# FFN in 512-token blocks, output projection and half of the convolution between its steps, one product for the head norms

## The chip, the cores and the metric

The kernel runs on one core of a Trainium2 chip. Its time is in device microseconds (us) of one execution. TensorE (PE) multiplies matrices and transposes, VectorE (DVE), ScalarE (ACT) and GpSimd (POOL) do elementwise work, and the queue of SyncE (SP) issues the DMA transfers.

## The reference

One layer of a streaming encoder, on 2048 prompt tokens and 32 tokens of a second stream that has 1024 cached tokens; model width 1024, all in float32.

```python
def layer(x, past_k, past_v, conv_state, ffn_state, ...):
    xn = rmsnorm(x, g_mix)
    q, k, v, u, gate = split(xn @ w_in)            # five times 512 columns
    q = head_rmsnorm(q, g_q); k = head_rmsnorm(k, g_k)   # 8 heads of 64
    o = sb_attend(q, k_all, v_all, ...)            # stick-breaking attention
    c = u * sigmoid(gate)
    c, new_conv_state = causal_dwconv(c, conv_state, w_dw, b_dw)   # 31 taps, 512 channels
    c = silu(layernorm(c, g_conv_ln, b_conv_ln))
    h = x + concatenate([o, c]) @ w_out            # 1024 x 1024
    up = rmsnorm(h, g_ffn) @ w_up                  # 1024 x 5632
    up_c, new_ffn_state = causal_dwconv(up, ffn_state, w_ffn_dw, b_ffn_dw)   # 3 taps
    a, g = split(up_c)                             # twice 2816
    y = h + (silu(g) * a) @ w_down                 # 2816 x 1024
    return y, k, v, new_conv_state, new_ffn_state
```

## The kernel before

Every matmul operand is split into a high part, rounded to float32r by ScalarE, and a low remainder, which VectorE gets by a subtraction (`split`). A product is three matmuls, high by high, high by low and low by high (`mm3`). All tiles lie in two large buffers, `arena` (float32) and `arena_r` (the split operands); `SLOTS` says where, by the name of a tile, and a name has as many buffers as it has places.

The order of the work isn't that of the code. Each helper (`mm`, `tr`, `act`, `vec`, `pool`, `dma`) adds a step to a list with an engine, an estimated price in ns and a rank, which is its place in the program unless one is set by hand. `Plan.run` then walks through time by these prices: an engine that is free takes the ready step of the lowest rank, and a step that opens one of the 8 banks of PSUM needs a free bank, which its rule for banks gives (the last bank only to the oldest tile). What comes out is one fixed stream for each engine, which takes its instructions in that order on the chip. All DMAs go through the queue of SyncE, also in that order. Since all engines' instructions are recorded in the helpers, a row shows the helper's line: L380 is a matmul, L387 a transpose, L394 ScalarE, L409 VectorE or GpSimd, L434 a DMA; the names of the tiles tell which step it is.

The stages, in the order of the program:
- Input projection, to about 565 us: the tokens' two halves, of each first u and gate (`ug`), then k, q and v (`nat`) in column tiles of 256. For q and k, `nat` squares (ScalarE), sums over a head (VectorE), takes the power -1/2 (GpSimd, `rstd_of`), scales each of 8 pieces of 64 columns by its norm (ScalarE, eight instructions), multiplies by the gain (GpSimd), splits and transposes. The gated u stays in `cb`, and `conv` runs the 31 taps on VectorE over 1024 tokens at a time. Its rank is set late, behind all attention, so that it fills VectorE's free time; by the trace it is done at about 564 us.
- Attention, to about 1096 us: `UNITS` of one head and 256 queries, with sigmoids on ScalarE, running products (scans) on VectorE and two matmuls on TensorE.
- Output projection, to about 1307 us: w_out is split once, into the `wo0` and `wo1` tiles; `out_chunk` then takes two token tiles of 128 at a time: reads the heads' output (oT_d) and the convolution (yT_d), normalises, multiplies, adds x and writes h to `h_d`. The last chunk has three tiles (the third is the second stream's 32 tokens), with the weights as the stationary side and a transpose behind.
- FFN, the rest: `SEGS` are 768, 640 and 640 + 32 tokens. `norm_seg` reads h back, scales it by norm and gain on VectorE, transposes and splits. For each of 22 tiles of 128 hidden columns `up` loads and splits two tiles of w_up (one for a, one for g), in every segment anew, multiplies in two column halves into two banks, runs the 3 taps on VectorE, SiLU, the product and a split, and loads and splits a tile of w_down. After each two of them `down` multiplies and adds to y.

## Time and profile before

| | before |
|---|---|
| runs | 2819.62 us median of 3 (2814.54 to 2824.38) |
| profiled execution | 2816.1 us, span 2814.2 us, mean granted clock 0.992 |
| busy | PE 2690.4 us (96%), DVE 2003.1 (71%), ACT 1103.1 (39%), POOL 494.3 (18%) |
| DMA | 288.29 MB, mean 102 GB/s |
| chain that ended last | PE 73%, DVE 10%, issue 6%, POOL 6%, ACT 3%, DMA 2% |

The span is the time from the first to the last instruction of the profiled execution; its own time is 1.9 us longer. Busy shares are means over stages that differ: which engine limits a stage is read from that stage's stretch. Idle time stands beside the engine whose result ended it.

### The profile page before, as it was taken

The page shows a single profiled execution, that of the slowest core. Times are in us where ns is not written, and L with a number is a line of the kernel's source. Part 1 is how long each engine was busy: PE and PEld are TensorE (multiplying, and loading weights), DVE is VectorE, ACT ScalarE, POOL GpSimd, SP SyncE. Part 2 cuts the span into 40 slices and gives each one's busy share as a digit, 9 for nine tenths or more (in the row PEclk, how much of TensorE's full clock was granted, in tenths as well). Part 3 has the DMA queues.
Part 4 walks back from the last instruction along what each step waited for, and adds up shares of the span by engine and source line. Part 5 has one row for each costly group of instructions (what it writes and reads, how often), then busy time and mean ns, then how long its engine had stood idle before and what let it go on. Part 6 is the DMA issues. An engine that isn't in the chain of part 4 may idle for free.

```text
span 2814.2 us, 43546 instructions
## 1 busy us (share of the span) xinstructions
PE 2690.4 (96%) x17345; PEld 2527.0 (90%) x17345; DVE 2003.1 (71%) x2311; ACT 1103.1 (39%) x2179; POOL 494.3 (18%) x724
## 2 busy tenths in 40 slices
PE   8999999988888888999999999999999999999999
PEld 8999999977777877889999999999999999999998
DVE  6988888899989998345565656666666665656566
ACT  5267235566666675114222222322232233322222
POOL 1155035523223231011000000000000001101100
PEclk9999999999999999999999999999999999999999
DMA  4255224644333335555222222242222233222221
GB/s 161 64 177 175 76 82 152 192 130 116 85 93 85 93 99 159 182 159 170 68 60 68 60 63 72 89 159 71 75 83 75 73 99 103 80 73 64 83 61 70
DMA packets 299907, 288.29 MB, mean 102 GB/s; under 512 B 21591, under 2 KB 260077, under 8 KB 298679
## 3 DMA queue, kind: packets, MB, share of 16 engines
q1 hardware_dynamic: 299703, 285.50, 33.3%
q8 instruction: 136, 2.23, 0.3%
q14 instruction: 68, 0.56, 0.1%
HBM read 217.08 MB, written 64.11 MB: 100 GB/s over the span
## 4 chain that ended last, share of the span: by engine, by line
PE 73%; DVE 10%; issue 6%; POOL 6%; ACT 3%; DMA 2%; SPq 0%; POOLq 0%; DVEq 0%; ACTq 0%
PE bank L380 70%; DVE arena L409 6%; POOL few L409 3%; DVE arena_r L409 3%; PE bank L387 3%; POOL arena L409 3%; ACT arena L394 2%; ACT arena_r L394 1%; DMA arena<-in_cache_sb_v_dram 1%; SPq L434 0%; DMA arena<-arena 0%; DVE few L409 0%; DMA oT_d<-arena 0%; DMA arena<-in_w_ffn_dw_dram 0%; DMA qT_d<-arena_r 0%
## 5 line engine op out<-in xcount | busy, mean ns | idle before, releaser
L380 PE MATMUL bank<-arena_r 128*128 128x256 f32 (+8 forms) x15360 | 2494.5, 322 | 32.4 <-DVE arena_r L409 31.0
L380 PEld LDWEIGHTS bank<-arena_r 128*128 128x128 f32 x15360 | 2320.6, 190 | 157.1 <-DVE arena_r L409 43.3
L409 DVE TENSOR_TENSOR arena_r<-arena,arena_r 128x1024 fp32r<-128x1024 f32 (+5 forms) x398 | 421.7, 1068 | 466.2 <-ACT arena_r L394 462.8
L394 ACT ACTIVATE arena_r<-arena 128x1024 fp32r<-128x1024 f32 (+5 forms) x398 | 368.7, 935 | 911.1 <-PE bank L380 509.8
L394 ACT ACTIVATE arena<-bank 128x384 f32<-128x384 f32 (+15 forms) x770 | 327.6, 473 | 278.2 <-PE bank L380 244.4
L409 DVE TENSOR_TENSOR arena<-bank,arena 128x512 f32<-128x512 f32 (+2 forms) x458 | 281.8, 631 | 189.5 <-PE bank L380 189.2
L409 DVE TENSOR_TENSOR_SCAN arena<-arena 128x1024 f32<-128x1024 f32 (+11 forms) x200 | 330.4, 1680 | 15.1 <-ACT arena L394 7.8
L409 DVE SCALAR_TENSOR_TENSOR arena<-arena,wdw 128x1024 f32<-128x1024 f32 (+1 forms) x240 | 320.6, 1367 | 1.6
L387 PE MATMUL bank<-ident,arena 128*128 128x128 f32 (+4 forms) x1645 | 224.0, 279 | 67.2 <-DVE arena L409 50.6
L387 PEld LDWEIGHTS bank<-ident,arena 128*128 128x128 f32 (+4 forms) x1645 | 185.5, 142 | 100.0 <-DVE arena L409 57.0
L409 POOL COPY halo<-arena 128x2 f32<-128x2 f32 x176 | 80.4, 472 | 1061.8 <-ACT arena L394 1049.8
L394 ACT ACTIVATE arena_r<-bank 128x512 fp32r<-128x512 f32 (+4 forms) x422 | 218.2, 570 | 110.5 <-PE bank L387 98.2
L409 DVE SCALAR_TENSOR_TENSOR arena<-arena,wfd 128x768 f32<-128x768 f32 (+2 forms) x264 | 248.1, 940 | 10.2
L409 DVE TENSOR_TENSOR arena_r<-bank,arena_r 128x512 fp32r<-128x512 f32 (+2 forms) x334 | 194.2, 634 | 18.2 <-ACT arena_r L394 18.0
L409 POOL TENSOR_SCALAR_AFFINE_SELECT arena<-arena 128x128 f32<-128x128 f32 (+1 forms) x130 | 132.8, 1032 | 338.5 <-ACT arena L394 338.1
L394 ACT ACTIVATE arena<-arena 128x1024 bf16<-128x1024 f32 (+4 forms) x100 | 88.2, 882 | 254.3 <-DVE arena L409 237.1
L409 POOL TENSOR_SCALAR few<-few 128x1 f32<-128x1 f32 (+3 forms) x87 | 62.1, 713 | 493.1 <-DVE few L409 405.3
L409 POOL TENSOR_TENSOR few<-few,nhalf 128x1 f32<-128x1 f32 (+3 forms) x87 | 112.0, 1290 | 6.6
L409 DVE TENSOR_TENSOR arena<-arena 128x768 f32<-128x768 f32 (+4 forms) x78 | 68.7, 881 | 46.7 <-ACT arena L394 33.2
L394 ACT ACTIVATE arena<-bank,few 128x64 f32<-128x64 f32 (+1 forms) x272 | 68.6, 325 | 77.9 <-POOL few L409 77.9
L409 DVE TENSOR_SCALAR arena<-arena,wfd,bfd 128x768 f32<-128x768 f32 (+2 forms) x132 | 84.0, 637 | 6.0 <-ACT arena L394 6.0
L409 POOL COPY arena<-halo 128x2 f32<-128x2 f32 x132 | 24.5, 185 | 294.1 <-DVE arena L409 281.7
(43 smaller groups left out, 377.8 us busy)
## 6 DMA issues: line engine op xcount, KB each, us to landing
arena<-in_w_up_dram SPq DMA_DIRECT2D x132, 512.0 KB
arena<-in_w_down_dram SPq DMA_DIRECT2D x66, 512.0 KB
arena<-in_x_prompt_dram SPq DMA_DIRECT2D x32, 512.0 KB
arena_r<-qT_d SPq DMA_DIRECT2D x64, 256.0 KB
arena<-h_d SPq DMA_DIRECT2D x32, 512.0 KB
arena<-in_w_in_dram SPq DMA_DIRECT2D x24, 512.0 KB
arena<-in_w_in_dram SPq DMA_DIRECT2D x32, 256.0 KB
out_dram<-arena SPq DMA_DIRECT2D x32, 256.0 KB
```

What stands on the lines that cost most here:

```text
L380: lambda: nc.tensor.matmul(plan.real(out), lhsT, rhs, start=start, stop=stop),
L387: "pe", in_.shape[0] * (0.4167 if in_.dtype == F32R else 0.8333) + 2.5, lambda: nc.tensor.transpose(plan.real(out), in_, idt), [out], [in_ ...
L394: "act", ns, lambda: nc.scalar.activation(out, plan.real(in_), func, **kw), aps(out, kw.get("accum_out")), reads
L409: self.tag, self.price(name, n / (2 if fast else 1), pointers), lambda: fn(out, *map(plan.real, args), **kw), [out], aps(*args, *kw.values())
```

## The change

- The FFN runs over four blocks of 512 tokens (`BLK`, `NBLK`); the second stream's 32 tokens go with the last. An up tile of the first three blocks is one bank of 512 columns, of the last two of 272. In the first block, weights are loaded raw in halves, split as before, and the split tiles stored to DRAM (`wu_d`, `wd_d`); the other blocks load these, 1 MB each.
- The output projection is cut into blocks and into its two halves of input rows: `project(b, 1, ...)` multiplies the convolution, `project(b, 0, ...)` the heads; the second to run adds to what the first wrote to h. Block 0 is projected between attention and FFN (convolution first). Block b + 1 is projected between the steps of block b's FFN, where a generator (`weave`, `upto`) adds its steps to the list (heads first). w_out is split anew in each of these, in the FFN's buffers (`out_weights`).
- The gated u goes to DRAM (`c_d`) instead of `cb`. `conv(b)` works on 512 tokens; blocks 0 and 1 in the input projection (rank behind all attention, as before), blocks 2 and 3 between the steps of the FFN's blocks 1 and 2.
- `norm_block` scales h by the norm on ScalarE, before the transposes, and by the gain (a column, `gff`) behind them, and needs all of its block.
- `nat` scales q and k by one VectorE product with broadcast norms.
- The planner: another price of matmuls and scans, and a rule for banks (`fits`, `pick`, `AHEAD`) that opens a bank early only where all older tiles would still get theirs. The FFN's small constants are loaded at the start.

In the changed kernel L415 is a matmul, L422 a transpose and L473 a DMA.

```diff
-SEGS = ((0, 768, 0), (768, 640, 0), (1408, 640, 32))
+BLK = 512
+NBLK = T // BLK
...
-    "raw4": spots(5120, 1024, 2),
+    "raw": spots(8192, 512, 4),
-    "wo0": [*spots(12288, 512, 4), *spots(20480, 512, 12)],
+    "wd": spots(20480, 2048, 3),
+    "wu": spots(16384, 2048, 2),
...
+        def fits(k):
+            if place[k] == oldest:
+                return True
+            if place[k] - oldest > AHEAD:
+                return False
+            before = [x for x in turn[oldest : place[k]] if x not in self.home]
+            held = [span[x] for x in open_] + [span[k]]
+            for x in before:
+                s = span[x][0]
+                need = sum(b >= s for _, b in held) + sum(span[y][0] <= s <= span[y][1] for y in before)
+                if need > len(self.banks):
+                    return False
+            return True
+        def pick():
+            for x in shut[:1]:
+                if fits(x[2]):
+                    return x
+            for x in shut:
+                if place[x[2]] == oldest:
+                    return x
+            return None
...
-            max(n * 0.4167, width(lhsT) * 0.8333) + 2.5,
+            max(n * 0.4167 + 13, 112),
...
+        return n * 2.1 + 50 if name == "tensor_tensor_scan" else n / 0.96 + 68 + 61 * pointers
...
+    def conv(b):
         for c in range(CT):
+            pieces = [(b * BLK, BLK)] + ([(T + 30, TS)] if b == NBLK - 1 else [])
+            for t0, m in pieces:
+                src = slot("csrc", (544,))[:, : m + 30]
+                need = ["c0"] + [("c", x) for x in {max(b - 1, 0), b}]
+                dma(src, c_d[c * P : (c + 1) * P, t0 : t0 + m + 30], gets=need)
+                acc = slot("cacc", (m,))
+                for k in (30, *range(30)):
+                    w = wdw[:, k * CT + c : k * CT + c + 1]
+                    if k == 30:
+                        vec.tensor_scalar(acc, src[:, k : k + m], w, cvec[:, c : c + 1], ALU.mult, ALU.add)
+                    else:
+                        vec.scalar_tensor_tensor(acc, src[:, k : k + m], w, acc, ALU.mult, ALU.add)
+                    yield
+                o = t0 if t0 < T else T
+                dma(yT_d[c * P : (c + 1) * P, o : o + m], acc, puts=[("y", b if t0 < T else NBLK)])
...
-        for i in range(nh):
-            act(kn[:rows, i], ph[:, i], AF.Copy, scale=r[:rows, i : i + 1])
+        vec.tensor_tensor(
+            kn[:rows, :nh], ph, r[:rows, :nh].unsqueeze(2).broadcast_to([rows, nh, HD]), ALU.mult
+        )
...
+    def out_weights(i):
+        nh, k = i // 4, i % 4 * 2
+        w = slot("wu", (2, 2, 512), F32R)
+        for j in range(2):
+            raw = slot("raw", (512,))
+            dma(raw, w_out[(k + j) * P : (k + j + 1) * P, nh * 512 : (nh + 1) * 512])
+            split(w[:, 0, j], w[:, 1, j], raw)
+        return w
...
+    def project(b, part, begin):
+        groups = [list(range(4 * b, 4 * b + 4))] + ([[16]] if b == NBLK - 1 else [])
+        for tl in groups:
+            w = sum(tokens(ti)[1] for ti in tl)
+            hi, lo = slot("cat", (CT, w), F32R), slot("cat", (CT, w), F32R)
+            for i in range(0, len(tl), 2):
+                some = tl[i : i + 2]
+                rs = slice(tokens(some[0])[0].start, tokens(some[-1])[0].stop)
+                cs = slice(i * P, i * P + rs.stop - rs.start)
+                fill = conv_out if part else heads_out
+                yield from fill(some, rs, rs.start // BLK, hi[:, :, cs], lo[:, :, cs])
+            for nh in range(2):
+                pss = [bank() for _ in tl]
+                for kk in range(2):
+                    wo = out_weights(4 * nh + 2 * part + kk)
+                    for i, ti in enumerate(tl):
+                        rows = tokens(ti)[1]
+                        for j in range(2):
+                            k = 2 * kk + j
+                            for n, (x, y) in enumerate(((hi, 0), (hi, 1), (lo, 0))):
+                                mm(
+                                    pss[i][:rows],
+                                    x[:, k, i * P : i * P + rows],
+                                    wo[:, y, j],
+                                    start=(k == 0 and n == 0),
+                                    stop=(k == CT - 1 and n == 2),
+                                )
+                    yield
+                for i, ti in enumerate(tl):
+                    rs, rows = tokens(ti)
+                    xt = slot("half", (512,))[:rows]
+                    if begin:
+                        dma(xt, x_prompt[rs, cs] if ti < 16 else x_sample[:, cs])
+                    else:
+                        dma(xt, h_d[rs, cs], gets=[("h1", ti, nh)])
+                    vec.tensor_tensor(xt, pss[i][:rows], xt, ALU.add)
+                    dma(h_d[rs, cs], xt, puts=[("h1", ti, nh) if begin else ("h", ti)])
...
+    def norm_block(b):
+        last = b == NBLK - 1
+        n = BLK + (TS if last else 0)
+        tag = "3" if last else ""
+        hh, hl = slot("hh" + tag, (KT, n), F32R), slot("hl" + tag, (KT, n), F32R)
+        tl = list(range(4 * b, 4 * b + 4)) + ([16] if last else [])
+        xs = []
+        for tix in tl:
             rs, rows = tokens(tix)
+            x = slot("tmp" if tix < 16 else "x5", (D,))
+            dma(x[:rows], h_d[rs, :], gets=[("h", tix)])
             ss = little()
             jk = slot("jk", (D,), BF16)
+            act(jk[:rows], x[:rows], AF.Square, accum_out=ss[:rows])
             r = rstd_of(ss[:rows], 1, rows, D)
+            act(x[:rows], x[:rows], AF.Copy, scale=r[:rows])
+            xs.append(x)
+        def out(k, ps, cs):
+            g = gff[:, k : k + 1]
+            act(hh[:, k, cs], ps, AF.Copy, scale=g)
+            vec.scalar_tensor_tensor(hl[:, k, cs], ps, g, hh[:, k, cs].bitcast(F32), ALU.mult, ALU.subtract)
+        for k in range(KT):
+            ps = bank()
+            for i in range(4):
+                tr(ps[:, i * P : (i + 1) * P], xs[i][:, k * P : (k + 1) * P], ident)
+            out(k, ps, slice(0, BLK))
...
+                if b == 0:
+                    for j in range(2):
+                        raw = slot("raw", (4, P))
+                        dma(raw, w_up_v[:, 4 * j : 4 * j + 4, fi * P : (fi + 1) * P])
+                        split(wu[:, 0, 4 * j : 4 * j + 4], wu[:, 1, 4 * j : 4 * j + 4], raw)
+                    dma(wu_d[fi], wu.rearrange("p a k n -> p (a k n)"), puts=[("wu", fi)])
+                else:
+                    dma(wu.rearrange("p a k n -> p (a k n)"), wu_d[fi], gets=[("wu", fi)])
+                ub = slot("ub" + tag, (2 + w,))
-                pss = [bank(), bank()]
+                pss = [bank() for _ in range(nc_)]
...
+    phase1()
+    attention()
+    mark = len(plan.steps)
+    for i, x in enumerate(convs):
+        x[4] = mark + i / len(convs)
+    normed = []
+    for part in (1, 0):
+        for _ in project(0, part, part):
+            pass
+    normed.append(norm_block(0))
+    for b in range(NBLK - 1):
+        work = []
+        if b:
+            work.append((conv(b + 1), n_conv[b + 1], 0.0, 0.6))
+        work.append((project(b + 1, 0, True), n_project(b + 1, 0), 0.1, 0.55))
+        work.append((project(b + 1, 1, False), n_project(b + 1, 1), 0.65, 0.97))
+        feed(b, weave(*work))
+    feed(NBLK - 1, lambda share: None)
```

TensorE's stream at the start of the FFN. Before: the last transposes are normalisation's for segment 0, and matmuls of 288 columns are the last chunk of the output projection.

```order
L380 MATMUL bank_61<-arena_r 128x288 x24
L380 MATMUL bank_63<-arena_r 128x288 x16
L387 MATMUL bank_62<-ident,arena 128x128 x4
L387 MATMUL bank_65<-ident,arena 128x128 x4
L380 MATMUL bank_63<-arena_r 128x288 x8
L380 MATMUL bank_60<-arena_r 128x288 x24
L380 MATMUL bank_58<-arena_r 128x288 x24
L387 MATMUL bank_61<-ident,arena 128x128 x4
L387 MATMUL bank_64<-ident,arena 128x128 x4
```

After: the first rows are the end of `project(0, 0, ...)`, then normalisation's eight times four transposes, then the first two up tiles.

```order
L415 MATMUL bank_63<-arena_r 128x512 x6
L415 MATMUL bank_62<-arena_r 128x512 x6
L422 MATMUL bank_60<-ident,arena 128x128 x4
L422 MATMUL bank_58<-ident,arena 128x128 x4
L422 MATMUL bank_65<-ident,arena 128x128 x4
L422 MATMUL bank_64<-ident,arena 128x128 x4
L422 MATMUL bank_59<-ident,arena 128x128 x4
L422 MATMUL bank_61<-ident,arena 128x128 x4
L422 MATMUL bank_63<-ident,arena 128x128 x4
L422 MATMUL bank_62<-ident,arena 128x128 x4
L415 MATMUL bank_60<-arena_r 128x512 x24
L415 MATMUL bank_58<-arena_r 128x512 x24
```

Matmuls of the output projection no longer stand between and behind normalisation's transposes: TensorE has nothing else there in its stream.

SyncE's queue at the same place. Before, the reads of h (by normalisation, and for y) and the last stores of h, then raw weights for the FFN:

```order
L434 DMA arena<-h_d 128x1024
L434 DMA h_d<-arena 128x1024
L434 DMA arena<-in_x_prompt_dram 128x1024
L434 DMA arena<-h_d 128x1024 x2
L434 DMA arena<-in_x_sample_dram 32x1024
L434 DMA arena<-h_d 128x1024 x7
L434 DMA h_d<-arena 128x1024 x2
L434 DMA h_d<-arena 32x1024
L434 DMA arena<-h_d 128x1024
L434 DMA arena<-in_w_down_dram 128x1024
L434 DMA arena<-in_w_up_dram 128x8x128 x2
```

After, the stores of h, the first block's raw weights and stores of split weights, and the reads of h:

```order
L473 DMA h_d<-arena 128x512 x3
L473 DMA arena<-in_w_up_dram 128x4x128
L473 DMA h_d<-arena 128x512
L473 DMA arena<-in_w_up_dram 128x4x128
L473 DMA wu_d<-arena_r 128x2048
L473 DMA arena<-in_w_up_dram 128x4x128
L473 DMA arena<-h_d 128x1024 x3
L473 DMA wd_d<-arena_r 128x2048
L473 DMA arena<-in_w_up_dram 128x4x128
L473 DMA arena<-h_d 128x1024 x5
```

Between the last store of h and the last read that normalisation needs, two stores of split weights have moved in.

In the middle of the FFN the queue before goes on with the last two rows of its fence, one raw tile of w_down to two of w_up. After, in a block into which projection and convolution are woven:

```order
L473 DMA yT_d<-arena 128x512
L473 DMA h_d<-arena 128x512
L473 DMA arena_r<-wd_d 128x2048 x2
L473 DMA arena<-c_d 128x542
L473 DMA arena_r<-wu_d 128x2048 x4
L473 DMA arena_r<-wd_d 128x2048 x2
L473 DMA arena_r<-wu_d 128x2048 x2
```

Loads of split weights stand where raw ones stood, with stores of h and of the convolution, and its input, between them.

## Rows read from the trace of the kernel before

**Rows 1.** The page: busy us (share of the span) and instructions of each engine.
```profile
PE 2690.4 (96%) x17345; PEld 2527.0 (90%) x17345; DVE 2003.1 (71%) x2311; ACT 1103.1 (39%) x2179; POOL 494.3 (18%) x724
```

**Rows 2.** Stretches: length; busy us (instructions); granted clock; DMA share, GB/s.
```profile
core 0: us, PE busy (x) PEld busy (x) DVE busy (x) ACT busy (x) POOL busy (x), PEclk, DMA share, GB/s
20.00:130.00 110.00, 108.60 (x904) 107.56 (x903) 91.01 (x100) 29.91 (x67) 9.07 (x11) 1.00 0.26 83
130.00:300.00 170.00, 160.21 (x1336) 155.65 (x1335) 146.79 (x163) 110.82 (x270) 87.96 (x63) 1.00 0.51 166
390.00:560.00 170.00, 157.72 (x1269) 154.32 (x1269) 144.86 (x139) 88.02 (x260) 100.70 (x68) 0.98 0.50 153
580.00:1095.00 515.00, 438.37 (x3067) 390.79 (x3065) 495.27 (x523) 345.30 (x725) 141.27 (x133) 0.98 0.35 97
1085.00:1090.00 5.00, 4.36 (x25) 4.36 (x26) 5.00 (x7) 2.54 (x5) 0.00 (x0) 0.66 0.28 97
1095.00:1115.00 20.00, 16.64 (x82) 13.57 (x81) 15.34 (x25) 12.50 (x20) 5.65 (x10) 0.91 0.93 246
1310.00:1800.00 490.00, 490.00 (x2626) 464.36 (x2625) 287.96 (x334) 131.65 (x186) 26.48 (x85) 1.00 0.23 69
```

**Rows 3.** Matmuls by form, 1310:1800, then 1840:2280: count, busy us, mean ns.
```profile
L380 PE MATMUL bank<-arena_r 128*128 128x384 f32 x1978 | 344.7, 334 | 0.0
L380 PE MATMUL bank<-arena_r 128*128 128x512 f32 x648 | 148.7, 390 | 0.0
...
L380 PE MATMUL bank<-arena_r 128*128 128x320 f32 x2062 | 304.0, 309 | 0.0
```

**Rows 4.** Instructions in time, two loads: start us, length us, engine, form [idle before].
```profile
996.07 0.32 SPq L434 DMA_DIRECT2D arena_r<-kT_d  x1
...
1531.62 0.34 SPq L434 DMA_DIRECT2D arena<-in_w_down_dram  x1
...
1535.04 1.06 ACT L394 ACTIVATE arena_r<-arena 128x1024 fp32r<-128x1024 f32 x1 [3.95 <-DMA arena<-in_w_down_dram]
```

**Rows 5.** Two microseconds of that load of keys (columns as rows 2).
```profile
998.00:999.00 1.00, 0.00 (x0) 0.00 (x0) 1.00 (x2) 0.20 (x1) 1.00 (x2) 1.00 0.98 360
999.00:1000.00 1.00, 0.90 (x9) 0.93 (x9) 1.00 (x2) 0.35 (x1) 1.00 (x3) 1.00 1.00 426
```

**Rows 6.** Groups by form, whole span: count, busy us, mean ns, idle before.
```profile
L409 DVE TENSOR_TENSOR arena_r<-arena,arena_r 128x1024 fp32r<-128x1024 f32 x260 | 317.2, 1222 | 419.4 <-ACT arena_r L394 416.3 <-PE bank L387 3.0
...
L409 DVE TENSOR_TENSOR arena<-bank,arena 128x512 f32<-128x512 f32 x354 | 239.4, 687 | 142.1 <-PE bank L380 141.9
...
L409 DVE SCALAR_TENSOR_TENSOR arena<-arena,wdw 128x1086 f32<-128x1086 f32 x120 | 165.9, 1413 | 0.8
...
L409 POOL TENSOR_TENSOR few<-few,nhalf 128x8 f32<-128x8 f32 x32 | 73.7, 2303 | 2.7
...
L394 ACT ACTIVATE arena<-bank,few 128x64 f32<-128x64 f32 x256 | 66.3, 327 | 75.8 <-POOL few L409 75.8
...
L409 DVE TENSOR_TENSOR arena_r<-arena,arena_r 128x512 fp32r<-128x512 f32 x64 | 44.1, 695 | 29.4 <-ACT arena_r L394 29.3
```

**Rows 7.** Waits, 20 to 565 us: who for whom, total us, times, longest.
```profile
ACT arena L394 <- POOL few L409: 80.4, 37, 6.5
...
PE bank L387 <- DVE arena_r L409: 20.4, 20, 2.3
```

**Rows 8.** Instructions in time, end of attention and start of the FFN.
```profile
1085.64 0.69 PE L387 MATMUL bank<-ident,arena 128*128 128x128 f32 x2 [2.66 <-DVE arena L409]
...
1283.30 0.33 SPq L434 DMA_DIRECT2D arena<-h_d  x1
...
1291.92 0.49 PE L387 MATMUL bank<-ident,arena 128*128 128x128 f32 x3
...
1307.02 1.14 PE L380 MATMUL bank<-arena_r 128*128 128x384 f32 x5 [1.07 <-DVE arena_r L409]
```

**Rows 9.** Chain that ended last, 190 to 200 us: start, length, what.
```profile
193.22 5.33 DMA qT_d<-arena_r
```

455 lines of the change are left out of this document (204 added, 251 removed).

## The prediction

> **What bounds the kernel now.** I read the page's busy shares, then a table by stretch, then matmuls by form and the waits inside a stretch. Over the span TensorE is busy 96% and VectorE 71% [rows 1]. The table says where each limits [rows 2]. From 1310 us on TensorE is busy 490.00 of 490 us and VectorE 287.96: in the FFN only TensorE's own work counts. In the attention (580 to 1095) VectorE is busy 495.27 of 515 us and TensorE 438.37: VectorE is the limit. In the stretches of the input projection that make q, k and v (130 to 300, 390 to 560) TensorE is busy 160.21 and 157.72 of 170 us. So the FFN pays only for fewer or cheaper matmuls, and loses by every new gap; the attention pays for VectorE work taken out; the projection has some stalls to give.
>
> **The FFN matmuls.** Busy time by count is 174.3 ns for 384 columns (344.7/1978), 147.4 for 320 (304.0/2062) and 229.5 for 512 (148.7/648) [rows 3]: 0.42 ns a column and 12.9 ns an instruction. Up-projection before: 44 column tiles x 24 products x 2 halves = 2112 per segment, 2112 x (174.3 + 147.4 + 154.1 for 336 columns) = 1004.9 us. After: 3 blocks x 1056 x 229.5 = 727.1, and in the last 2112 x 127.2 (272 columns) = 268.7, together 995.8: **-9**. The down-projection keeps its instructions. The Trainium skill ("TensorE: Matmul & The Clock Gate", section "Wait — 56ns, not 53.3ns?") gives a warm matmul its columns at 2.4 GHz and about 2.5 ns fixed; by that 1056 fewer instructions would save 2.6 us in place of 9. The rows decide: the fixed part is five times as large here.
>
> **Weights split once.** Three quarters of the FFN lose the splits of w_up and w_down on ScalarE and VectorE: worth 0, since TensorE waits for nothing there [rows 2]. In their place come 1 MB loads of split weights into two buffers. TensorE mostly runs four up tiles in a row; the third's load can start when the first's 24 matmuls end and has to land within the next 24 x 229.5 ns = 5.5 us. What a load takes: 512 KB of w_down is issued at 1531.62 and its split starts at 1535.04, 3.42 us [rows 4]. A 1 MB load of keys, issued at 996.07 [rows 4], moves 360 and 426 GB/s in its full microseconds [rows 5], so another 512 KB adds some 1.3 us. Estimate 4.7 us for 1 MB, 0.8 to spare; with 512 KB queued in front it is 0.5 late. There are 2 such loads per pair of FFN tiles x 11 x 3 blocks = 66. If a third of them finds something in front, 22 x 0.5 = 11, and some 4 us for the block starts, where stores of y and loads of x, h and the heads' output share the queue: **+15**. Bounds: 0 (none late) and 60 (half of them 1.8 late, behind a whole MB). The first block, which still splits and also stores 3 MB per FFN tile, lies inside them: 4.7 MB in its 72 x 229.5 ns = 16.5 us is 286 GB/s, below those rows.
>
> **q and k.** Eight scalings by ScalarE of 327 ns, 2.6 us in a row, become one VectorE product of some 687 ns, as its other 128x512 reads of PSUM take [rows 6]. The product still stands behind GpSimd's power (2.3 us [rows 6]), for which ScalarE waited 80.4 us [rows 7]; VectorE will now. But VectorE loses half of the convolution from this stage: 120 steps of 1.41 us [rows 6] = 166 us of low-ranked work, which the transposes' inputs stood behind (20.4 us of TensorE's waits [rows 7]). At the pace of 20 to 130 us (904 matmuls in 110 us) the 1336 and 1269 of the two stretches would take 162.6 and 154.4 us in place of 340 together [rows 2]: 23 at most. I take half, **-11**; bounds -23 and, if VectorE waiting for GpSimd delays weight splits, +8.
>
> **Attention.** No convolution ran here, so none leaves. Of the splits from SBUF 12 leave with w_out's, at 0.69 us [rows 6] = 8 us of VectorE, and its 20 us of idle time [rows 2] may shrink with the planner's new price of a scan: **-10**; bounds 0 and -28.
>
> **The end of the attention.** Today TensorE is busy 16.64 of the 20 us from 1095, at a granted clock of 0.91 [rows 2]: about 5 us lost. After, the load of the first two tiles' convolution output goes into a buffer that the last unit's products occupy, and behind the last attention matmul stand that load (3.4 us as above), statistics, power, normalisation, transposes, SiLU and split. With the load half hidden and some 0.7 us for each of the others with its latency, half of it beside its neighbour, I count 10 us lost: **+5**, bounds 0 and +12.
>
> **The start of the FFN.** Today normalisation's reads run under the output projection's last matmuls and the first FFN matmul waits about a microsecond [rows 8]. After, norm_block(0) needs all of block 0 and nothing else is ready, as the order shows. Its chain: addition 0.7; store of h 3.4 at least (as a 512 KB load; a 512 KB store of q stood in the chain with 5.33 [rows 9]); read of h to the first transposes, 1283.30 to 1291.92 = 8.6 us [rows 8]; copy and split of the first tile 1.3. Sum 14.0. Two 1 MB stores and three 512 KB reads stand in the queue before the last token tile's read, 2.6 and 1.3 us each at the rate of [rows 5]; the first of them pass while the store of h is under way, I add 6: **+20**, bounds 11 and 24. A cold clock follows (0.66 in 1085 to 1090 [rows 2], behind a wait of 2.66 us [rows 8]): +2.
>
> **Output projection.** 816 matmuls of 512 columns for 672 of 512 and 192 of 288 (134 ns by the line above): 187.3 - 154.2 - 25.7 = 7, less 24 transposes: **+5**. Its repeated splits and additions and half of the convolution now lie under the FFN. VectorE's share there stays near today's 59%: two thirds of the splits go (317.2 us over all 1024-wide ones [rows 6]), 166 us of convolution and some 60 of the projection come.
>
> **Sum.** -9 + 15 - 11 - 10 + 5 + 20 + 2 + 5 = +17 on the profiled execution's 2816.1 us (span 2814.2) is 2833. The runs' median is 3.5 us above that execution and their lowest 1.6 below; the terms are no finer than that, and I say **2831**.
>
> **Rivals.** (1) Faster: the planner's order holds in the FFN as it does now. Loads 0, projection -20, attention -22, end of attention 0, start of FFN +13, the rest -4: 2783 at best, 2805 halfway from the forecast's 2831. For it: a full TensorE in the FFN today. Against it: no load had to land within 5.5 us. (2) Slower by far: weight loads late throughout. It decides from the point where 1 MB takes over 5.5 us from release to use; with 512 KB in front of each of the 66 it costs 33 in place of 15, with a whole MB 119, so I price it at 60: 2876. For it: one queue carries everything in order, and a waiting store holds up the loads behind it. Against: 4.7 us alone. The Trainium skill ("DMA: Bandwidth & Descriptors", section "Bandwidth") lists 6.15 us of engine time for 1 MB, measured on GpSimd's path; by it 66 x 0.65 = 43 us would be lost and the time be 2859. The rates of [rows 5] speak against its figure here. (3) The projection gets slower: VectorE, which takes its instructions in order, stands behind GpSimd's power 32 times with three short convolution steps before it in the first half and none in the second; +8 for -11 gives 2850. Against it: VectorE, busy 144.86 of 170 us there, is relieved of the 166. (4) No saving per instruction, since columns alone count: 2840, the forecast's side.
>
> **Chances.** Forecast (with 4) 0.47, its own range 2815 to 2850; rival 1 0.29; rival 2 0.16; rival 3 0.08. Leaving out the ends of 1 and 2, 8 in 10 lie between 2788 and 2872. Within 0.3% of 2819.6, about what a measurement can tell from no change, is 2811 to 2828. Faster: 0.22 of rival 1 and 0.04 of the forecast. Same: 0.07 of rival 1, 0.13 of the forecast, 0.01 of rival 3. Slower: the remaining 0.53.
>
> **What would show it.** Right: TensorE busy 99% of the FFN, one hole of 15 to 24 us between output projection and first up tile; an attention some 10 us shorter with VectorE over 96%; over 7.9 matmuls per us where q, k and v are made; up matmuls at 229 ns. Wrong: many gaps of TensorE put down to loads of wu_d (rival 2); VectorE waiting over 60 us for GpSimd in the projection (rival 3); a first up tile within 8 us of the output projection (rival 1). An attention made longer by the planner's new rule for banks would make the account itself wrong.

## The result and the profile after

The changed kernel takes 2947.11 us (median, 2944.53 to 2949.41), before 2820.43: a ratio of 1.0451 (95% interval 1.043 to 1.0471). 2831 was forecast, with a range that ended at 2872. The profiled execution has a span of 2945.5 us, 131.3 more than before. The busy row of the page, as [rows 1]:

```profile
PE 2722.0 (92%) x16218; PEld 2417.5 (82%) x16218; DVE 2031.1 (69%) x2915; ACT 993.7 (34%) x1924; POOL 453.3 (15%) x809
```

TensorE is busy only 32 us longer, so 100 of the 131 us are idle time. The table by stretch, columns as in [rows 2]:

```profile
130.00:300.00 170.00, 152.54 (x1235) 147.71 (x1235) 142.62 (x197) 85.01 (x147) 75.03 (x62) 0.97 0.49 156
390.00:560.00 170.00, 163.73 (x1341) 161.01 (x1341) 98.53 (x136) 62.71 (x118) 68.76 (x62) 0.99 0.48 149
580.00:1105.00 525.00, 454.93 (x3101) 416.05 (x3100) 497.73 (x527) 336.73 (x724) 154.95 (x142) 0.93 0.32 87
1105.00:1219.00 114.00, 61.34 (x245) 49.12 (x246) 38.38 (x54) 34.25 (x51) 4.46 (x12) 0.72 0.63 205
1105.00:2945.50 1840.50, 1725.43 (x8764) 1471.25 (x8764) 1151.20 (x1861) 441.86 (x808) 136.99 (x501) 0.97 0.63 222
```

And the same of before for all that follows its attention, whose last matmul ends at 1095.75:

```profile
1096.00:2814.20 1718.20, 1708.03 (x9896) 1603.57 (x9896) 1018.08 (x1284) 485.40 (x784) 143.33 (x420) 1.00 0.30 92
```

The attention now ends at 1104.8, 9 us later. Behind it come 1840.5 us in place of 1718.2, 122 more: 105 of them idle (115.1 against 10.2), 17 busy. What TensorE waits for there (engine and tile, for whom, total us, times, longest):

```profile
PE bank L415 <- DMA arena_r<-wu_d: 44.3, 18, 14.3
PE bank L422 <- ACT arena L429: 28.1, 5, 16.5
PE bank L415 <- ACT arena_r L429: 26.3, 6, 17.8
PE bank L415 <- DVE arena L444: 5.6, 3, 2.7
PE bank L422 <- DMA arena<-yT_d: 2.3, 1, 2.3
PE bank L422 <- DVE arena L444: 1.9, 2, 1.6
PE bank L415 <- DVE arena_r L444: 0.7, 2, 0.4
```

That is 109 us in 37 waits. The first block's path is most of the second and third row. TensorE in time, from the convolution's half of the first projection to the first up tile (start, length, [idle before <- what ended it]):

```profile
1107.12 1.97 PE L422 MATMUL bank<-ident,arena 128*128 128x128 f32 x8 [2.31 <-DMA arena<-yT_d]
...
1117.87 24.75 PE L415 MATMUL bank<-arena_r 128*128 128x512 f32 x96 [2.97 <-ACT arena_r L429]
1160.38 24.00 PE L415 MATMUL bank<-arena_r 128*128 128x512 f32 x96 [17.76 <-ACT arena_r L429]
1200.90 0.47 PE L422 MATMUL bank<-ident,arena 128*128 128x128 f32 x1 [16.52 <-ACT arena L429]
1209.47 0.47 PE L422 MATMUL bank<-ident,arena 128*128 128x128 f32 x1 [8.09 <-ACT arena L429]
...
1213.65 5.85 PE L422 MATMUL bank<-ident,arena 128*128 128x128 f32 x29 [2.66 <-ACT arena L429]
1219.26 22.02 PE L415 MATMUL bank<-arena_r 128*128 128x512 f32 x96
```

Between the halves it idles 17.76 us, and normalisation's reads of h leave it idle for 16.52 + 8.09 + 2.66 = 27.3. The chain that ended last, at the start of block 1 (start, length, what):

```profile
1632.77 13.86 DMA arena<-oT_d
...
1646.69 10.82 DMA arena_r<-wu_d
...
1657.56 4.64 PE bank L415 x10
```

and in the last block, where nothing is woven in:

```profile
2584.34 6.86 DMA arena_r<-wu_d
2591.20 0.14 issue
2591.33 0.73 PE bank L415 x4
```

At a block's start the first weight load stands behind eight reads of the heads' output in the queue, and then takes 10.82 us itself; TensorE waits 14.28 us there and 12.92 at block 2. The load of 6.86 us has something in front too: the queue shows two loads of w_down, 1 MB each, issued 4.4 and 4.0 us before it. A load with nothing under way ahead is issued at 2597.61 (queue, then table by stretch):

```profile
2579.93 0.80 SPq L473 DMA_DIRECT2D arena_r<-wd_d  x2
2597.61 0.32 SPq L473 DMA_DIRECT2D arena_r<-wu_d  x1
2597.60:2602.60 5.00, 5.00 (x42) 5.00 (x42) 2.14 (x3) 0.69 (x3) 0.31 (x2) 1.00 0.59 210
```

All of its megabyte (210 GB/s for 5 us) has moved 5 us after the issue. By the trace's records of landings 58 of the 132 loads of wu_d have nothing ahead of them, and their median from issue to landing is 4.9 us; nine of ten take less than 5.3. The nine in the last block that stand behind two loads of w_down take 6.0 to 7.4. What a wait leaves behind, in the table by stretch:

```profile
1645.00:1650.00 5.00, 0.00 (x0) 0.00 (x0) 2.00 (x3) 0.63 (x1) 0.00 (x0) 0.54 1.14 228
1650.00:1655.00 5.00, 0.00 (x0) 0.00 (x0) 3.99 (x5) 1.57 (x2) 0.00 (x0) 0.50 1.05 315
1655.00:1660.00 5.00, 2.44 (x6) 1.98 (x7) 1.23 (x1) 1.06 (x1) 0.00 (x0) 0.50 1.01 406
1660.00:1665.00 5.00, 5.00 (x19) 4.00 (x18) 0.00 (x0) 0.00 (x0) 0.00 (x0) 0.75 0.88 324
1665.00:1670.00 5.00, 5.00 (x24) 4.14 (x23) 2.06 (x3) 0.60 (x1) 0.51 (x2) 1.00 0.67 227
```

The granted clock falls to half, the lower of its two levels (1.2 and 2.4 GHz), while TensorE stands, and is still at 0.75 after it has gone on: 19 matmuls in 5 us, where 24 pass at the full clock in the next row. In the busy time of the rows from 1655 to 1665 that is some 2.5 us lost (half of 2.44 and a quarter of 5.00, an estimate), behind a wait of 14.28. Up matmuls themselves are as forecast: 1265 of 512 columns, 228.1 ns each, in a stretch of block 0 without a wait (288.6 us by form).

### The profile page after: what moved, and what is told of

It reads as the page before. It is cut to its first block, busy times and chain, and to the rows that moved or that the text cites. A ratio compares the mean times of both kernels' runs of the same rounds, so it can differ in the third digit from the quotient of the medians.

```text
span 2945.5 us, 42693 instructions
## 1 busy us (share of the span) xinstructions
PE 2722.0 (92%) x16218; PEld 2417.5 (82%) x16218; DVE 2031.1 (69%) x2915; ACT 993.7 (34%) x1924; POOL 453.3 (15%) x809
## 2 busy tenths in 40 slices
DMA packets 277157, 538.25 MB, mean 183 GB/s; under 512 B 31535, under 2 KB 181453, under 8 KB 242135
## 4 chain that ended last, share of the span: by engine, by line
PE 60%; DVE 11%; DMA 9%; ACT 2%; issue 2%; POOL 1%; SPq 1%; DVEq 0%; POOLq 0%; ACTq 0%
PE bank L415 57%; DVE arena L444 7%; DMA arena_r<-wu_d 4%; DVE arena_r L444 4%; PE bank L422 3%; DMA arena<-oT_d 1%; ACT arena_r L429 1%; ACT arena L429 1%; SPq L473 1%; DMA arena<-arena 1%; DMA wu_d<-arena_r 1%; POOL arena L444 1%; DMA arena<-h_d 1%; DMA h_d<-arena 0%; DMA arena<-in_cache_sb_v_dram 0%
## 5 line engine op out<-in xcount | busy, mean ns | idle before, releaser
L415 PE MATMUL bank<-arena_r 128*128 128x512 f32 (+7 forms) x14256 | 2530.8, 337 | 110.8 <-DMA arena_r<-wu_d 44.3
L415 PEld LDWEIGHTS bank<-arena_r 128*128 128x128 f32 (+1 forms) x14256 | 2204.3, 192 | 382.9 <-DVE arena_r L444 36.0
L429 ACT ACTIVATE arena<-bank 128x512 f32<-128x512 f32 (+12 forms) x715 | 324.3, 501 | 1001.4 <-PE bank L415 928.1
L429 ACT ACTIVATE arena_r<-arena 128x512 fp32r<-128x512 f32 (+2 forms) x420 | 286.6, 691 | 456.4 <-PE bank L415 163.6
L444 DVE TENSOR_TENSOR arena<-bank,arena 128x512 f32<-128x512 f32 (+4 forms) x488 | 308.3, 638 | 180.4 <-PE bank L415 169.7
L444 DVE TENSOR_TENSOR arena_r<-arena,arena_r 128x512 fp32r<-128x512 f32 (+2 forms) x420 | 316.5, 765 | 150.7 <-ACT arena_r L429 146.0
L444 DVE SCALAR_TENSOR_TENSOR arena<-arena,wdw 128x512 f32<-128x512 f32 (+1 forms) x600 | 406.4, 677 | 11.5
L444 DVE TENSOR_TENSOR_SCAN arena<-arena 128x896 f32<-128x896 f32 (+10 forms) x200 | 329.6, 1683 | 2.8 <-POOL arena L444 1.8
L422 PE MATMUL bank<-ident,arena 128*128 128x128 f32 (+4 forms) x1622 | 236.2, 287 | 85.0 <-ACT arena L429 39.8
L422 PEld LDWEIGHTS bank<-ident,arena 128*128 128x128 f32 (+4 forms) x1622 | 194.9, 148 | 111.8 <-ACT arena L429 46.9
L444 DVE SCALAR_TENSOR_TENSOR arena<-arena,wfd 128x512 f32<-128x512 f32 (+1 forms) x352 | 266.4, 757 | 10.4
L429 ACT ACTIVATE arena_r<-bank 128x512 fp32r<-128x512 f32 (+3 forms) x388 | 204.2, 573 | 159.1 <-PE bank L422 145.2
L444 DVE TENSOR_TENSOR arena_r<-bank,arena_r 128x512 fp32r<-128x512 f32 (+2 forms) x300 | 176.2, 630 | 12.9 <-ACT arena_r L429 12.5
L422 PE MATMUL bank<-identr,arena_r 128*128 128x128 f32 (+1 forms) x336 | 35.5, 249 | 22.1 <-DVE arena_r L444 22.1
```

The source lines that it names most:

```text
L415: lambda: nc.tensor.matmul(plan.real(out), lhsT, rhs, start=start, stop=stop),
L422: "pe", in_.shape[0] * (0.4167 if in_.dtype == F32R else 0.8333) + 2.5, lambda: nc.tensor.transpose(plan.real(out), in_, idt), [out], [in_ ...
L429: "act", ns, lambda: nc.scalar.activation(out, plan.real(in_), func, **kw), aps(out, kw.get("accum_out")), reads
L444: self.tag, self.price(name, n / (2 if fast else 1), pointers), lambda: fn(out, *map(plan.real, args), **kw), [out], aps(*args, *kw.values())
```

## The experiments

### The first block's path and the queue

half_apart takes away the sharing of buffers between the rows of h on their way (`half`) and what the heads' output is read into (`tmp`).

```diff
-    "half": spots(4096, 512, 8),
+    "half": spots(18944, 512, 8),
```

> The changed kernel, with the half-row tiles of the output projection (half) in places of their own, so that they share none with tmp, into which the heads' output is read. Theory A (the 17.8 us hole between the two halves of the first block's projection is a wait for buffers: the reads of the heads' output need tmp places that half still holds until its stores of h are done): hole under 8 us, 2930 to 2938 us. Theory B (the reads stand in the queue behind the other transfers anyway): hole over 14 us, within 0.2% of 2947.

2943.36 us, ratio to before 1.0439 (1.0415 to 1.0463). The hole between the halves fell from 17.76 to 1.46 us, so it was the buffers. But the gain was 4 us, not 9 to 17: the first up tile began at 1198.89 in place of 1219.26, 20 us sooner, and the FFN gave 16 back. TensorE's waits for wu_d rose from 44.3 to 56.6. Theory A had the place right and the worth wrong.

heads_held holds back the heads' reads at the start of a block.

```diff
-                    gets=[("o", blk)],
+                    gets=[("o", blk)] + ([("up", blk - 1)] if ("up", blk - 1) in plan.keys else []),
...
+                if f == 3 and part:
+                    plan.keys[("up", b)] = [len(plan.steps) - 1]
...
-        work.append((project(b + 1, 0, True), n_project(b + 1, 0), 0.1, 0.55))
+        work.append((project(b + 1, 0, True), n_project(b + 1, 0), 0.2, 0.6))
```

> The changed kernel, with the reads of the heads' output for the next block held back until the fourth hidden tile of a block is out (and that half of the projection spread over 0.2 to 0.6 of the block in place of 0.1 to 0.55). Theory A (the 14.3 and 12.9 us gaps at the starts of blocks 1 and 2 are the first 1 MB weight load waiting behind eight reads of the heads' output): both gaps under 4 us, and with the clock that fell behind them 2905 to 2920 us. Theory B (y stores, h reads and a 1 MB load that takes 10 us would make the gap alone, or the held reads make it later in the block): gaps over 8 us at the starts or in mid-block, 2935 us or more.

2933.54 us, 1.041 (1.0391 to 1.0428), 13.6 less than the changed kernel. The gaps of 14.3 and 12.9 are 3.1 and 3.3 now, as A said. Yet the waits for wu_d are as long in sum:

```profile
PE bank L415 <- DMA arena_r<-wu_d: 44.9, 24, 4.5
```

They come 24 times, 4.5 us at most, where they came 18 times. Moving the reads took the waiting away from the block starts, and it came back inside the blocks; the time lies between the two theories. Nor do the 13.6 us come from these waits. Behind 1225 us TensorE idles 52.4 us for 62.4, and nearly all of the 10 us are waits for VectorE and ScalarE (12.2 us there in the changed kernel, here 2.6); its busy time is 3 us less. Why those waits went was not tried.

raw_each_block takes the split weights' way through DRAM out.

```diff
-                if b == 0:
+                if True:
...
-                    dma(wu_d[fi], wu.rearrange("p a k n -> p (a k n)"), puts=[("wu", fi)])
...
-            if b == 0:
+            if True:
...
-                dma(wd_d[f], wd.rearrange("p a n -> p (a n)"), puts=[("wd", f)])
```

> The changed kernel, but every FFN block loads raw weights in halves and splits them, as its first block does; nothing is stored to or loaded from wu_d and wd_d. Theory A (the stores and 1 MB loads of split weights fill the one queue): the 44 us of TensorE's waits for wu_d go, the hole of 28 us before the first up tile shrinks to some 17 because the reads of h no longer stand behind two 1 MB stores, and fewer cold stretches follow: 2865 to 2890 us in place of 2947. Theory B (the queue is held up by the heads' reads and the other small transfers, and the splits load VectorE): the same gaps come back at the block starts, put down to raw weights or to VectorE: 2925 us or more.

2918.71 us, 1.0352 (1.0333 to 1.037): 28 less, between the theories and nearer to B. Normalisation's hole fell from 27.3 to 21.0 us (10.45, 7.85 and 2.65) and all waits for wu_d went. In their place TensorE waits for VectorE, up to 10.0 us at a time. Over the run 365.34 MB move in place of 538.25, and VectorE is busy 2249.3 us in place of 2031.1, since it splits weights in every block.

raw_held_apart makes the three edits at once.

> The changed kernel with three edits at once: raw weights loaded and split in every block, the heads' reads held back, and half in places of its own. Alone they brought 28, 14 and 4 us. Theory A (each takes away another wait, and the queue is relieved by all): 2945 less 45 to 65, 2880 to 2902 us. Theory B (with the raw weights VectorE is the limit in blocks 1 and 2, and the two others gain nothing there): 2908 us or more.

2904.83 us, 1.0305 (1.029 to 1.0321): 42 less, some 3 short of the sum of the three (46), between the theories and close to A. B is right about what is left. All of TensorE's waits over 1.2 us in the FFN lie in blocks 1 and 2, and all are for VectorE's splits. The sum behind 1200 us, and a stretch of block 2:

```profile
PE bank L415 <- DVE arena_r L444: 42.2, 13, 6.8
```

```profile
2090.00:2190.00 100.00, 88.77 (x367) 72.13 (x368) 91.30 (x186) 32.79 (x53) 8.13 (x19) 0.93 0.52 145
```

VectorE is busy 91% there, with the convolution's steps between the others; the longest gap, VectorE first, then TensorE:

```profile
2109.39 0.24 DVE L444 SCALAR_TENSOR_TENSOR arena<-arena,wdw 128x32 f32<-128x32 f32 x1
2109.55 0.54 DVE L444 TENSOR_SCALAR arena<-arena,wfd,bfd 128x512 f32<-128x512 f32 x1
2110.01 0.24 DVE L444 SCALAR_TENSOR_TENSOR arena<-arena,wdw 128x32 f32<-128x32 f32 x1
...
2119.31 0.24 DVE L444 SCALAR_TENSOR_TENSOR arena<-arena,wdw 128x32 f32<-128x32 f32 x1
2119.47 0.68 DVE L444 TENSOR_TENSOR arena_r<-arena,arena_r 128x512 fp32r<-128x512 f32 x1
...
2120.20 2.07 PE L415 MATMUL bank<-arena_r 128*128 128x512 f32 x4 [6.82 <-DVE arena_r L444]
```

A step of the convolution stands before each other instruction, and the split for which TensorE waits 6.82 us behind them all.

### The convolution under the FFN

In two kernels the convolution of blocks 2 and 3 is cut to one tap.

```diff
-                for k in (30, *range(30)):
+                for k in (30, *range(30 if b < 2 else 0)):
```

> The changed kernel, in which the convolution of blocks 2 and 3 leaves out 30 of its 31 taps, so that some 360 short VectorE steps are missing under the FFN of blocks 1 and 2. Theory A (these steps, which the prediction gave no price, hold up what TensorE waits for in those blocks): 2915 to 2930 us. Theory B (in the changed kernel those blocks are limited by the loads of split weights, and VectorE has room): within 0.3% of 2947.

> raw_held_apart (2905 us) with the same 30 taps left out in blocks 2 and 3. Theory A (VectorE, which splits the weights there in every block, is held up by the convolution's steps: TensorE's gaps of 43 us lie in the two blocks with it and nowhere else): gaps in the FFN below 12 us, 2845 to 2865 us. Theory B (the splits and additions of the woven output projection do it): gaps over 30 us, 2885 us or more.

In the changed kernel it brings 6 us (2940.67, 1.0432, 1.0414 to 1.045): B. TensorE waits 46.9 us for wu_d, as it did. In raw_held_apart it brings 62 (2842.96, 1.0084, 1.007 to 1.0098): A, and a little more than it said. In the FFN, TensorE's waits are 0.8 us in sum. From the first up tile to the end, with all taps and then with one:

```profile
1190.26:2902.40 1712.14, 1663.50 (x8518) 1424.40 (x8516) 1332.87 (x2203) 636.56 (x1153) 168.68 (x491) 0.99 0.41 125
1192.96:2842.00 1649.04, 1643.05 (x8519) 1414.44 (x8517) 1167.25 (x1843) 635.13 (x1153) 138.38 (x491) 1.00 0.43 129
```

That is 63 us: 43 of idle time, and 20 of busy time for the same matmuls, as the granted clock goes from 0.99 to 1.00. So the gaps are two thirds of the gain, and the clock behind them the other third. The same steps cost 6 us in one kernel and 62 in the other. But the two differ in more than the late loads: raw_held_apart also splits the weights of every block, and VectorE is busy 2253.0 us in it for 2031.1. What the steps would cost beside split weights that arrive in time was not tried.

raw_held_apart_conv sends that convolution, whole, back to the input projection, with a rank behind all attention.

```diff
-                    else:
-                        mark = len(plan.steps)
-                        for b in range(2):
+                    mark = len(plan.steps)
+                    for b in (2 * half, 2 * half + 1):
...
-        if b:
-            work.append((conv(b + 1), n_conv[b + 1], 0.0, 0.6))
```

> raw_held_apart (2905 us) with the convolution of blocks 2 and 3 back in the input projection (its rank behind all attention, as for blocks 0 and 1), so that none is woven into the FFN. Theory A (VectorE's gaps of 43 us in blocks 1 and 2 come from short convolution steps that stand before weight splits in its stream; the prediction gave this work no price): TensorE's waits for VectorE's splits in the FFN fall below 15 us, 2855 to 2880 us. Theory B (the splits of w_out and the additions of the woven projection do it, or the convolution costs as much in the projection stage): 2890 us or more.

2958.31 us, 1.0493 (1.0478 to 1.0509): 53 slower than raw_held_apart, in B's range. FFN blocks 1 and 2 are full (TensorE busy at least 98.9 us of every 100 from 1400 to 2900), so A's cause holds; but the steps cost more where they went. Some came at the worst place, at the start of the attention:

```profile
614.36 14.90 DVE L444 SCALAR_TENSOR_TENSOR arena<-arena,wdw 128x512 f32<-128x512 f32 x19
632.56 0.55 DVE L444 TENSOR_SCALAR arena<-arena,wdw,cvec 128x512 f32<-128x512 f32 x1 [3.30 <-DMA arena<-c_d]
633.14 23.59 DVE L444 SCALAR_TENSOR_TENSOR arena<-arena,wdw 128x512 f32<-128x512 f32 x30
...
660.16 1.11 PE L422 MATMUL bank<-ident,arena 128*128 128x128 f32 x4 [46.75 <-DVE arena L444]
```

The planner put some 50 low-ranked steps here, which by its rule it does only where VectorE has nothing else to do in its account of time. On the chip, where streams are fixed, TensorE waited 46.75 us for what came behind them. And 236 of the 372 steps ran neither in the projection nor under the attention, but behind its end, from 1155 us on, beside the first block's path: from 1200 to 1400 TensorE was busy 134.8 of 200 us, with VectorE at 174.4.

raw_held_apart_spread leaves them in the FFN, but thinner and earlier.

```diff
-        if b:
-            work.append((conv(b + 1), n_conv[b + 1], 0.0, 0.6))
+        if b < 2:
+            work.append((conv(b + 2), n_conv[b + 2], 0.0, 0.95))
```

> raw_held_apart (2905 us) with the convolution of blocks 2 and 3, all its taps, spread thinner and earlier: that of block 2 over the FFN of block 0, that of block 3 over nearly all of block 1, none in block 2. With the taps left out it took 2843 us. Theory A (the steps cost because they come dense: VectorE is busy over 90% of the stretches with gaps and 70% of block 0): TensorE's waits for splits in the FFN fall from 43 us below 20, 2868 to 2885 us. Theory B (any convolution step in the FFN stands before a split that TensorE needs, so that it costs wherever it is put): gaps over 35 us, 2895 us or more.

2854.38 us, 1.0123 (1.01 to 1.0147): 50 of the 62 us with all taps, more than A asked. TensorE's waits for splits in the FFN fall to 6.6 us. In block 0 VectorE is now busy 365.76 of 410 us, TensorE 408.99; in block 1, where w_out's splits and additions stand beside the steps as they did, VectorE is busy 394.30 of 440 us (1610 to 2050) and TensorE 430.62. So a share of 89 or 90% alone does no harm. Why the thinner order spares TensorE's splits isn't shown by these runs.

### The planner

before_new_plan is the kernel before with the new planner: the two price lines of the change's diff, and `fits` and `pick`. before_new_rule has only the rule, before_mm_price the rule and the matmul's price.

> The kernel before with the planner of the changed one alone: its rule for banks and its prices of matmuls and scans. Theory A (the attention, which ends some 9 us later in the changed kernel, is slower because of the planner's other order): 2826 to 2834 us, the attention 8 to 12 us longer. Theory B (it ends later for what follows it, or for the missing w_out splits' places and the convolution): within 0.2% of 2820.

> The kernel before with the planner's new rule for banks alone, at its old prices. The kernel before with rule and prices took 2861 us in place of 2819. Theory A (the rule does it: a bank is opened early only if all older tiles would still get theirs, so that matmuls which are ready wait): 2852 to 2865 us. Theory B (the prices do it, by another order of steps on all engines): 2815 to 2828 us.

> The kernel before with the new rule for banks and the new price of a matmul, but the old price of a scan. Rule and both prices took 2861 us, the rule alone 2821. Theory A (the matmul's price, which moves the whole projection and what VectorE does in its gaps): 2845 us or more. Theory B (the scan's price, which is too far from the measured 2.3 us for 1024 columns or moves the convolution): within 0.3% of 2820.

2861.13 us (1.0148, 1.013 to 1.0165), 2820.65 (1.0006, 0.9996 to 1.0015) and 2873.4 (1.0186, 1.017 to 1.0201). The rule does nothing, the matmul's price costs 53 us, the scan's gives 12 back. Neither theory on before_new_plan held: not the attention is longer, but the projection slower (its last store of q is issued at 589 us, in the kernel before at 550). From 20 to 567 us before_new_rule does 4252 matmuls, before_mm_price 4036, and there:

```profile
PE bank L423 <- DVE arena_r L445: 40.2, 25, 5.1
```

against 22.3 us with the rule alone. A price nearer to the measured duration made the order worse. Why it does was not tried.

before_new_plan_nat adds the product to before_new_plan (its edit is in the change's diff).

> The kernel before with the changed kernel's planner (2861 us) and its one VectorE product per query or key tile in place of eight ScalarE scalings. Theory A (the product is worth half of what the projection loses, as the prediction's term has it, less the part that the moved convolution would bring): 2850 to 2858 us. Theory B (TensorE's inputs wait for VectorE, which takes one more instruction and a wait for GpSimd): 2861 to 2872 us.

2854.46 us, 1.0127 (1.0112 to 1.0142): 6.7 less than before_new_plan; the intervals of the two ratios overlap a little. Theory A's range holds it.

after_old_plan gives the changed kernel the old planner, after_old_prices the old prices alone.

> The changed kernel with the planner of before (rule for banks and prices). Theory A (the planner costs the changed kernel in the projection what it costs the kernel before, where the product and the absent convolution hid it): projection some 20 to 30 us shorter, 2905 to 2928 us. Theory B (with less VectorE work in the projection the new planner does no harm there, and the old one, which knows no cost of a matmul's start, does worse in the FFN): 2940 us or more.

> The changed kernel with the planner's new rule for banks, but at the old prices of matmuls and scans. With old rule and prices it took 2960 us, its attention ended 12 us earlier and its FFN took longer. Theory A (the prices cost the attention 11 us here as they cost the kernel before 40, and the rule is what the FFN needs): 2928 to 2940 us. Theory B (the prices are what the woven FFN's order needs, and what they take from the attention they give back there): 2950 to 2965 us.

2960.22 us (1.0499, 1.0481 to 1.0516) and 2955.97 (1.0481, 1.0462 to 1.0499): slower than the changed kernel, theory B both times. But with the old prices the output projection's first transposes begin 12 us sooner:

```profile
1095.20 1.09 PE L422 MATMUL bank<-ident,arena 128*128 128x128 f32 x8 [1.53 <-DMA arena<-yT_d]
```

in place of 1107.12. So the new prices cost 12 us up to there, and save 21 behind it. What they cost lies in the projection, whose last store of q is issued 21 us later with them. The old prices, the new ones, and the kernel before:

```profile
531.53 0.37 SPq L469 DMA_DIRECT2D qT_d<-arena_r  x1
552.29 0.38 SPq L473 DMA_DIRECT2D qT_d<-arena_r  x1
549.35 1.35 SPq L434 DMA_DIRECT2D qT_d<-arena_r  x2
```

### The FFN matmuls alone

before_512 has four segments of 512 tokens in the kernel before.

```diff
-SEGS = ((0, 768, 0), (768, 640, 0), (1408, 640, 32))
+SEGS = ((0, 512, 0), (512, 512, 0), (1024, 512, 0), (1536, 512, 32))
...
-                pss = [bank(), bank()]
+                pss = [bank() for _ in range(nc_)]
```

> The kernel before with FFN segments of 512, 512, 512 and 512 + 32 tokens, one column part in the first three, and nothing else changed (weights are loaded and split four times in place of three). Theory A (1056 matmuls fewer at 12.9 ns each, the columns unchanged, and VectorE has room for the fourth pass): 2806 to 2814 us. Theory B (columns alone count, or a fourth pass of splits makes TensorE wait): 2817 us or more.

2952.97 us, 1.0475 (1.0455 to 1.0495), for a reason that neither theory had. Under the old rule for banks the first segment's matmuls come one group at a time, each behind a wait until the one before is read out. From 1310 to 1800 us that is 117 waits and 105 us in sum, such as this:

```profile
1411.58 1.66 PE L380 MATMUL bank<-arena_r 128*128 128x512 f32 x6 [0.78 <-DVE arena L409]
```

before_512_nat adds the new rule and the product, before_512_rule the new rule alone.

> before_512 with the one VectorE product per query or key tile, and with the new rule for banks at the old prices (the rule alone changes nothing; without it the order with the product can't be planned). Theory A (both are worth here what they are worth alone, 9 and 7 us): 2798 to 2808 us, less than both kernels. Theory B (with the old prices the product's wait for GpSimd costs what it saves): within 0.2% of before_512.

> The kernel before with FFN segments of 512 tokens (before_512, 2953 us) and the new rule for banks at the old prices. Before_512_nat, with the product too, took 2841 us, 24 of them in one stall of its attention. Theory A (with the rule the stall over single banks is gone and 1056 fewer matmuls bring 9 us): 2806 to 2814 us. Theory B (what the fewer matmuls save, a fourth segment's start and its weights take): within 0.2% of 2820. Theory C (the order of the attention falls badly here too): 2830 us or more.

before_512_nat takes 2840.67 us (1.0074, 1.0062 to 1.0087): its FFN is mended by the new rule, but one wait of 23.4 us at the start of the attention has VectorE in ten steps of the convolution, as above. before_512_rule takes 2811.57 (0.9971, 0.9959 to 0.9982): 8 us less than before, as theory A had it, and the fastest of all, ahead of both kernels.

## Why the prediction was wrong

**The FFN matmuls, -9: right.** before_512_rule has 8.2 us, net of a fourth pass of splits. An up matmul took 228.1 ns for 229.5. Rival 4 is out. By the 2.5 ns fixed that the Trainium skill gives a matmul ("TensorE: Matmul & The Clock Gate", section "Wait — 56ns, not 53.3ns?") it would have been 2.6 us.

**Weights split once, +15: mis-sized.** The duration of a load was right: 4.7 us put together from [rows 4, 5], and 4.9 measured with nothing ahead. The step that failed is what stands in front of it. For the block starts I had "some 4 us" in all; two of them cost 14.28 and 12.92, behind the eight reads of the heads' output. In mid-block I let a third of the loads be 0.5 us late behind 512 KB, 11 us; 16 waits cost 17 there, and those of the last block stand behind 2 MB. From issue to landing 35 of the 132 loads took over 5.5 us, the prediction's mark for rival 2, and it named many gaps put down to wu_d as a sign of being wrong: there are 18, of 44.3 us. The Trainium skill's 6.15 us for 1 MB ("DMA: Bandwidth & Descriptors", section "Bandwidth") is engine time on GpSimd's path, and it is not borne out on this queue: the 4.9 us from issue to landing are less. And the whole term was an account of single loads, while half_apart's gain came back for the most part as other waits for wu_d (12 us more), and heads_held moved them without making them less. Only where raw_each_block cut the bytes in the queue by a third were they gone, which speaks for the queue's time as a whole.

**The end of the attention and the start of the FFN, +5 and +20 (+2 of clock): mis-sized, and a term missing.** Ahead of the projection's first matmul TensorE idles 7.2 us, within the 10 that I had counted. Normalisation's reads cost 27.3 for 20; raw_each_block puts 6 of these down to the stores of split weights, as many as I had added for them, so the chain itself took 21 in place of 14. The step that failed most has no term: the 17.76 us between the two halves, where I followed the data and not the buffers. TensorE waits 53 us in this stretch.

**The clock, +2: mis-sized.** Forecast were 2 us less of busy time behind the attention (-9 + 5, and +2 of clock), measured are 17 more. So some 21 us (an estimate, from these numbers) are matmuls at the lower clock, about half of them in the first block's path, where the granted clock was 0.72 in the mean. To 105 us of idle time the clock adds a fifth.

**q and k, -11, and attention, -10: both failed.** The projection's last matmul did not move (566 us, 567 before) and the attention ended 9 us later. The product itself took 691 ns for 687 (32 of them, 22.1 us) and VectorE stood 34 us before it for GpSimd, as rival 3 had it, whose bound of 60 it didn't reach. The step that failed: the planner's new prices were no term of the sum, but for a gain that I put down to the scan's. before_new_plan shows what they can do (41 us in all), after_old_prices that 12 of the 30 us missed are theirs. With them the first half of the projection did 101 matmuls fewer than before in 130 to 300 us [rows 2], the second 72 more. At the old prices the forecast gain is there: the last store of q is issued at 531.53 us, in the kernel before at about 550. The product alone does little for it: 556.1 in before_512_nat for 556.6 in before_512_rule, at the same rule and prices. So the 25 us from there go with the halved convolution and what else the change moved out of this stage; that wasn't taken apart. In the attention the idle time of VectorE, which I had shrinking, grew to 27.3 us (525.00 less 497.73) from 19.7, with a granted clock of 0.93 for 0.98. It waits for ScalarE's rounded parts, from 580 on (after, before):

```profile
DVE arena_r L444 <- ACT arena_r L429: 16.1, 27, 3.3
DVE arena_r L409 <- ACT arena_r L394: 4.1, 8, 0.9
```

Whether order or clock does that was not tried, and the other 18 us stay open.

**Output projection under the FFN, at nothing: right in the changed kernel, for the wrong reason.** VectorE's share didn't "stay near today's 59%", it was 71% from 1310 to 1800 (346.45 of 490 us) and 65% from 1225 to the end (1109.99 of 1720.50). The convolution's steps cost 6 us there (after_tap), where the loads are late; in raw_held_apart, whose loads are not and where VectorE also splits weights, they cost 62.

In sum, -21 up to the attention's end became +9, and +38 behind it became +122. raw_held_apart_tap, which leaves 30 taps of two blocks out, is still 23 us above the kernel before. Most of that is the first block's path: its first up tile begins at 1192.96, with 192 projection matmuls done since about 1102, and TensorE waits 31 us in between.

## What to carry to other kernels

Work that is woven under a full engine is free only as long as the engines and the queue that feed it have room in that stretch: give each woven step a price there, and try an edit on more than one variant, since its worth can depend on the rest (6 us in one kernel, 62 in another for the same steps). Before a duration is called a transfer's own, look at what the queue had under way ahead of it (4.9 us alone, 6.0 to 7.4 behind two others). A fixed order from estimated prices is a part of the change: price its edit as one, by the order that it gives, and look for low-ranked work that stands in front of what the critical engine needs.

## What the runs showed of the hardware

A 1 MB load into 128 partitions, with nothing under way ahead of it in the queue, took 4.9 us from issue to landing (median of 58 in the changed kernel), 6.0 to 7.4 behind two 1 MB loads issued some 4 us before, and 10.82 behind reads of the heads' output. While these passed, the DMA engines were fully busy (a share of 1.14) at 228 GB/s; in the load's own time, from 1655, they moved 406 (the table by stretch above). TensorE's clock was granted at half within the 5 us in which it stood, and the rows after its next matmul (1657.56) show 0.75, and 1.00 from 1665 on.
